# Stick-breaking scans with their second operand in a PSUM bank, and one projection bank in place of two

## Chip, cores and metric

The kernel runs on one core of a Trainium2 chip. The metric is the device time of one execution in microseconds (us): the median of 3 runs was 3153.06 us, from 3152.79 to 3157.4. A core has a matrix engine (TensorE, PE in the profile, with its weight loads as PEld), VectorE (DVE), ScalarE (ACT), GpSimd (POOL) and DMA queues that SyncE (SP) and others feed. Each engine works through its own instructions in order and waits on semaphores for the others. SBUF is the on-chip memory. PSUM is the matrix engine's output memory, eight banks of 512 float32 values on each of 128 partitions; VectorE and ScalarE reach it as well.

## What is computed

One decoder layer on 2048 tokens of width 1024, all in float32: modulated RMSNorm, one input projection, forgetting attention on 8 heads beside stick-breaking attention on 8 heads, output projection, then a channel mixer of an up-projection, a causal convolution of width 3, SiLU gating and a down-projection. The change lies in the stick-breaking attention:

```python
def stick_breaking_attention(q, k, v):
    """A[t,s] = sigmoid(z_ts) * prod_{s<j<t} (1 - sigmoid(z_tj)), s < t, in log space. q,k,v: (B,H,S,Dh)."""
    ...
        z = jnp.einsum('bhqd,bhkd->bhqk', q_blk, k, preferred_element_type=jnp.float32) * scale
        strict = kpos[None, :] < qpos[:, None]
        log_one_minus_beta = jnp.where(strict, jax.nn.log_sigmoid(-z), 0.0)
        rest = lax.cumsum(log_one_minus_beta, axis=3, reverse=True) - log_one_minus_beta
        log_a = jax.nn.log_sigmoid(z) + rest
        a = jnp.where(strict, jnp.exp(log_a), 0.0)
        return jnp.einsum('bhqk,bhkd->bhqd', a.astype(v.dtype), v)
```

For each query row the product of the factors 1 - sigmoid(z) runs from the diagonal to the left. The kernel forms it with a scan over the keys in reversed order.

## The kernel before

**Units.** The attention is cut into 32 units: stick-breaking ("sb") head pairs 0 to 3 with four token blocks of 512 each are units 0 to 15, forgetting ("fox") ones units 16 to 31. A unit has two things to do. Its *projection* (`proj`, `finish_proj`) makes q, k and, for even head pairs, v of two pairs. Its *attention* (`Unit`, `Head`, `SbItem`, `Group`) goes through the unit's queries against all earlier keys.

**Projection.** q and k are each one accumulation group of 24 matmuls of 512 columns (`accumulate`, L268) into a bank that `pj()` hands out; v is two groups of 48 matmuls of 256 columns (L310). A finished group is read from its bank first by ACT (a copy that rounds to the matrix format, L278 or L44) and then by DVE (the remainder, L279 or L45), for V twice each. Only then is the bank free. Pool `psa` has two such banks, so one group can be read out while the next accumulates.

**Stick-breaking attention.** For each head, each of two 128-row query blocks and each chunk of up to 512 keys, `SbItem.weights` does: two matmuls for the logits into a `qk` bank (L368, L369); two sigmoids on ACT, one into a row strip `rw` and one into `a` (L457, L458); the scan on DVE over `rw`, from right to left, in place; and the product `a * rw` shifted by one on POOL (L471). The head's last chunk holds the diagonal (L463): its second operand is the constant `edge`, which is zero but for an identity matrix in its last 128 columns, and the operation is multiply and then maximum, so that the running product starts at 1 on each row's diagonal. Every other chunk (L466) starts from the neighbour's leftmost value and only multiplies; the second operation is "bypass", and the second operand, which doesn't enter the result, is `rw` itself. `Group.turn` then transposes `a` on PE (L383) into a `pt` bank, ACT and DVE read it out (L387, L388), and `Group.add` multiplies with V on PE (L398).

**The stage.** Units 0 to 2 are attended with short strips (`r`); units 3 to 15 follow with `long_rows` set, in one call of `attend`, which looks up to two items ahead, while `fill_proj` advances the projections of units 4 to 16 in step with the attention. After it the fox stage begins with `attend(plan[16:], 2, 2)`. PSUM then holds `psb` (2 `qk`, 3 `pt`, 1 `pv`) and `psa` (2 `pj`). The order in which instructions stand on each engine is not that of the code alone: the framework's scheduler places them by priority and by its own estimate of when each is ready, buffers included, so a change in the number of buffers moves instructions on every engine.

Of the kernel before, what the change touches and what calls it, by code (L numbers as in the profile page):

```python
# [11 lines left out]
AF = mybir.ActivationFunctionType  # L12
ALU = mybir.AluOpType
PSUM = bass.MemoryType.PSUM
# [9 lines left out]
TB = 512  # L24
# [9 lines left out]
def kernel(ctx: ExitStack, tc: tile.TileContext, x, c, w_ada, b_ada, g_attn, w_in, b_fgate,  # L34
                      g_out_fox, g_out_sb, w_out, g_mlp, w_up, conv_w, conv_b, w_down, g_final, out):
    nc = tc.nc
# [28 lines left out]
    edge = const.tile([P, TB + 1], F32, name="edge")  # L65
# [67 lines left out]
    def open_pool(name, side=None, space=None):  # L133
        st = pools[name] = ExitStack()
        kw = dict(space=space) if space is not None else {}
        return st.enter_context(tc.tile_pool(name=name, bufs=1, side=side, reuse_waits="tile", **kw))

    def close_pool(*names):
        for name in names:
            pools.pop(name).close()  # L140

    psb = open_pool("psb", space=PSUM)
    psa = open_pool("psa", side="right", space=PSUM)
# [5 lines left out]
    def bank(pool, tag, bufs):  # L149
        return pool.tile([P, 512], F32, name=f"ps_{tag}", tag=tag, bufs=bufs)  # L150

    pj = lambda: bank(psa, "pj", 2)
    qk = lambda: bank(psb, "qk", 2)
    pt = lambda: bank(psb, "pt", 3)
    pv = lambda: bank(psb, "pv", 1)
# [210 lines left out]
    def logits(cw, qcols, hl, Q, K):  # L366
        b = qk()
        nc.tensor.matmul(b[:, :cw], Q[:, hl, 0, qcols], K[:, hl, :cw], start=True, stop=False)  # L368
        nc.tensor.matmul(b[:, :cw], Q[:, hl, 1, qcols], K[:, hl, :cw], start=False, stop=True)  # L369
        return b  # L370
# [57 lines left out]
    class SbItem:  # L428
# [14 lines left out]
        def weights(self, qi):  # L443
            head, ch = self.head, self.ch
            last = ch == head.n - 1
            need = min(512, (2 * head.j + qi + 1) * P - ch * 512)
            b = logits(max(need, 2 * P), head.qcols(qi), head.hl, head.Q, head.K[ch])
            if last:
                head.right = getattr(head, "right", [None, None])
                if long_rows:  # L450
                    head.right[qi] = sx.tile([P, S + 1], F32, name="rw", bufs=3)
            if long_rows:
                r = head.right[qi][:, ch * 512:ch * 512 + need + 1]
            else:
                r = sx.tile([P, 512 + 1], F32, name="r", bufs=7)
            self.at[qi] = a = sx.tile([P, 512], F32, name="a", bufs=7)
            nc.scalar.activation(r[:, :need], b[:, :need], AF.Sigmoid)  # L457
            nc.scalar.activation(a[:, :need], b[:, :need], AF.Sigmoid, scale=-1.0)  # L458
            if last:

                nc.gpsimd.memset(r[:, need:need + 1], 0.0)
                rev = r[:, 0:need + 1][:, ::-1]
                nc.vector.tensor_tensor_scan(rev, rev, edge[:, TB - need:TB + 1][:, ::-1], 0.0, ALU.mult, ALU.max)  # L463
            elif long_rows:
                rev = r[:, 0:need][:, ::-1]
                nc.vector.tensor_tensor_scan(rev, rev, rev, r[:, need:need + 1], ALU.mult, ALU.bypass)  # L466
            else:
                nc.gpsimd.tensor_copy(r[:, need:need + 1], head.right[qi][:, 0:1])
                rev = r[:, 0:need + 1][:, ::-1]
                nc.vector.tensor_tensor_scan(rev, rev, rev, 1.0, ALU.mult, ALU.bypass)  # L470
            nc.gpsimd.tensor_mul(a[:, :need], a[:, :need], r[:, 1:need + 1])  # L471
            if not long_rows:
                head.right[qi] = r
# [290 lines left out]
    def fill_proj(target, limit=len(units)):  # L764

        while stock and made[0] < limit and taken[0] < target:
            if next(stock[0], StopIteration) is StopIteration:
                stock.pop(0)
                made[0] += 1
                continue  # L770
            taken[0] += 1
# [24 lines left out]
    def unit_proj(i):  # L796
        yield from proj_gen(units[i], xt0 if i == 0 else None)

    psc = p2a = ex = None
    wo = []  # L800
    stock = [unit_proj(i) for i in range(len(units))]
    taken = [0]
# [4 lines left out]
    sx = open_pool("sx", side="right")  # L807
# [8 lines left out]
    ex = open_pool("ex", side="right")  # L816
    sx = open_pool("sx", side="right")
    long_rows = True
    base = taken[0]
    goal = 0  # L820
    seen = {}
# [8 lines left out]
    tick(1 << 20)  # L830
    while made[0] <= 16:
        fill_proj(taken[0] + 1)
    close_pool("sx", "ex")
    ex = None
    sx = open_pool("fx", side="right")
    base = taken[0]
    seen = {}
# [270 lines left out]
    for tb in range(NTB):  # L1108
# [21 lines left out]
        for t in range(4):  # L1130
# [4 lines left out]
            r = de.tile([P, 1], F32, name="r_f", bufs=4)  # L1135
# [43 lines left out]
```

## Time and profile before

| quantity | value |
|---|---|
| median of 3 runs | 3153.06 us |
| span of the profiled execution | 3151.1 us, 1.96 us under the median |
| mean granted TensorE clock in the span | 0.979 |
| PE busy in the span | 2971.6 us (94%), 15934 matmuls |
| DVE busy | 2138.4 us (68%) |
| ACT busy | 1655.3 us (53%) |
| POOL busy | 1306.8 us (41%) |
| stick-breaking stage of units 3 to 15 | 268 to 906.5 us |

The profile is of one execution, whose own time is known by its span alone; the 1.96 us beside it are the distance to the median of the runs. In a row for a group of instructions stand the line, the engine, the operation, output and inputs by the program's names, the shapes and the count, then the busy time in us and the mean of one in ns, and behind a second bar the idle time of the engine just before them with what ended it. A row of waits reads: who waited for whom, us in all, times, longest. A row of stretches gives the busy time of each engine from one point to another, with the number of instructions, and then the granted clock, the share of the DMA engines and GB/s. A row of the timeline begins with start and duration in us. Matmuls are pipelined and their ends are modelled, so a row of several matmuls runs a little into the next; distances from start to start are the ones to use.

### The profile page before, as it was taken

How to read it: one execution, taken by the hardware profiler on the slowest of the kernel's cores; microseconds unless marked ns; L12 is line 12 of the kernel's file. 1: busy time of each engine (PE TensorE's matmuls, PEld its weight loads, DVE VectorE, ACT ScalarE, POOL GpSimd, SP SyncE). 2: the span in 40 equal slices, each digit the busy share in tenths (PEclk: the TensorE clock that was granted, in tenths of full speed). 3: DMA queues.
4: the chain of work that ended last, by engine and by line, in shares of the span. 5: the costliest groups of instructions: out<-in, count | busy, mean ns of one | idle time of the engine just before them, and what ended most of it. 6: DMA issues, size and time to landing. Idle time of an engine off the chain costs nothing.

```text
span 3151.1 us, 46387 instructions
## 1 busy us (share of the span) xinstructions
PE 2971.6 (94%) x15934; PEld 2517.7 (80%) x15934; DVE 2138.4 (68%) x3422; ACT 1655.3 (53%) x3033; POOL 1306.8 (41%) x1459
## 2 busy tenths in 40 slices
PE   7889898989989999999999999999899998999998
PEld 5778797878878889887877778888678887888887
DVE  6776689787976776556743577777987776254253
ACT  5565577666765565556743444444544444343332
POOL 2673566666653242242212244444444442332321
PEclk8999999999999999999999999999999999999999
DMA  9439633654236685685546632222222223554552
GB/s 266 169 133 300 193 106 97 215 180 134 76 115 213 219 288 180 185 301 169 170 153 219 213 96 85 83 88 85 84 81 82 87 86 123 190 201 158 192 200 90
DMA packets 292939, 496.51 MB, mean 158 GB/s; under 512 B 29448, under 2 KB 177664, under 8 KB 291680
## 3 DMA queue, kind: packets, MB, share of 16 engines
q1 hardware_dynamic: 281072, 480.92, 47.9%
q10 hardware_dynamic: 11632, 12.63, 1.1%
q8 instruction: 126, 2.06, 0.3%
q14 instruction: 109, 0.89, 0.1%
HBM read 352.61 MB, written 90.51 MB: 141 GB/s over the span
## 4 chain that ended last, share of the span: by engine, by line
PE 51%; DVE 14%; DMA 13%; POOL 9%; issue 7%; ACT 4%; SPq 2%; POOLq 0%; DVEq 0%; ACTq 0%
PE ps_pj L268 8%; PE ps_o L1118 8%; PE ps_pv L398 6%; PE ps_pt L383 5%; PE ps_pj L310 5%; PE ps_o L968 4%; PE ps_t L1118 4%; PE ps_bc L1118 4%; DMA wuraw<-in_w_up_dram 3%; PE ps_qk L368 3%; DVE wu L45 3%; PE ps_qk L369 3%; DMA hp<-hs 2%; DVE u L1037 2%; POOL ws L956 2%
## 5 line engine op out<-in xcount | busy, mean ns | idle before, releaser
L968 PE MATMUL ps_o<-oa,wu 128*128 128x512 f32 x2088 | 502.7, 392 | 12.6 <-DVE oa L45 5.8
L968 PEld LDWEIGHTS ps_o<-oa,wu 128*128 128x128 f32 x2088 | 391.1, 188 | 102.5 <-DVE oa L45 9.6
L398 PE MATMUL ps_pv<-at,V 128*128 128x256 f32 x2304 | 437.8, 300 | 21.3 <-DVE at L388 8.8
L388 DVE TENSOR_TENSOR at<-ps_pt,at 128x512 fp32r<-128x512 f32 (+1 forms) x576 | 365.1, 650 | 122.4 <-ACT at L387 119.6
L268 PE MATMUL ps_pj<-hp,w_qk 128*128 128x512 f32 x1512 | 417.2, 407 | 17.7 <-DMA hp<-hs 5.5
L387 ACT ACTIVATE at<-ps_pt 128x512 fp32r<-128x512 f32 (+1 forms) x576 | 319.1, 576 | 193.0 <-PE ps_pt L383 132.5
L471 POOL TENSOR_TENSOR a<-a,rw 128x512 f32<-128x512 f32 (+2 forms) x272 | 317.2, 1176 | 234.8 <-DVE rw L466 68.3
L398 PEld LDWEIGHTS ps_pv<-at,V 128*128 128x128 f32 x2304 | 341.8, 192 | 57.9 <-DVE at L388 18.5
L268 PEld LDWEIGHTS ps_pj<-hp,w_qk 128*128 128x128 f32 x1512 | 276.2, 192 | 73.6 <-DMA hp<-hs 7.2
L45 DVE TENSOR_TENSOR wd<-wdraw,wd 128x1024 fp32r<-128x1024 f32 x88 | 112.7, 1280 | 261.9 <-ACT wd L44 261.8
L45 POOL TENSOR_TENSOR g<-graw,g 128x512 fp32r<-128x512 f32 x84 | 142.7, 1702 | 325.8 <-ACT g L44 325.8
L368 PE MATMUL ps_qk<-K,Q 128*128 128x512 f32 (+2 forms) x640 | 260.7, 408 | 14.9 <-ACT a L458 7.1
L466 DVE TENSOR_TENSOR_SCAN rw<-rw 128x512 f32<-128x512 f32 x168 | 251.4, 1509 | 18.0 <-ACT rw L457 16.9
L1118 PE MATMUL ps_o<-wd,g 128*128 128x512 f32 x1040 | 251.1, 391 | 8.7 <-ACT g L44 8.7
L968 PE MATMUL ps_t<-ob,wu 128*128 128x512 f32 x984 | 244.0, 393 | 0.0
L310 PE MATMUL ps_pj<-w_v,hp 128*128 128x256 f32 (+1 forms) x1536 | 230.8, 293 | 9.8 <-DVE V L45 4.6
L369 PE MATMUL ps_qk<-K,Q 128*128 128x512 f32 (+2 forms) x640 | 236.7, 371 | 0.0
L1118 PEld LDWEIGHTS ps_o<-wd,g 128*128 128x128 f32 x1040 | 196.2, 189 | 49.9 <-ACT g L44 9.1
L44 ACT ACTIVATE wu<-wuraw 128x512 fp32r<-128x512 f32 x214 | 133.2, 626 | 195.8 <-PE ps_o L968 132.4
L383 PE MATMUL ps_pt<-edge,a 128*128 128x128 f32 x1088 | 189.8, 280 | 43.0 <-POOL a L471 37.5
L310 PEld LDWEIGHTS ps_pj<-w_v,hp 128*128 128x128 f32 x1536 | 209.8, 195 | 17.3 <-issue 8.7
L968 PEld LDWEIGHTS ps_t<-ob,wu 128*128 128x128 f32 x984 | 187.0, 190 | 39.4 <-ACT hf_m L873 0.2
(222 smaller groups left out, 5753.7 us busy)
## 6 DMA issues: line engine op xcount, KB each, us to landing
hp<-hs SPq DMA_DIRECT2D x224, 512.0 KB
wuraw<-in_w_up_dram SPq DMA_DIRECT2D x84, 512.0 KB
wdraw<-in_w_down_dram SPq DMA_DIRECT2D x84, 512.0 KB
Q<-q SPq DMA_DIRECT2D x128, 256.0 KB
g<-u SPq DMA_DIRECT2D x42, 512.0 KB
graw<-g SPq DMA_DIRECT2D x84, 256.0 KB
hs<-hp SPq DMA_DIRECT2D x32, 512.0 KB
K<-q SPq DMA_DIRECT2D x128, 128.0 KB
```

Of the source, the lines that this page charges most:

```text
L45: (lo_engine or nc.gpsimd).tensor_sub(lo, src, f(hi))
L268: nc.tensor.matmul(acc, w[kt][:, a, n], h[:, bb], start=kt == 0 and i == 0, stop=kt == KT - 1 and i == 2)
L310: nc.tensor.matmul(av[:, t * width:(t + 1) * width], hts[kt][:, a, tok], w[1][kt][:, bb, 0:width], start=kt == 0 and m == 0, stop=kt == KT ...
L368: nc.tensor.matmul(b[:, :cw], Q[:, hl, 0, qcols], K[:, hl, :cw], start=True, stop=False)
L369: nc.tensor.matmul(b[:, :cw], Q[:, hl, 1, qcols], K[:, hl, :cw], start=False, stop=True)
L383: nc.tensor.transpose(b[:, i * P:(i + 1) * P], self.blk(self.kts[kk], qi), ident)
L387: nc.scalar.activation(at[:, 0, lo:], b[:, lo:], AF.Copy)
L388: nc.vector.tensor_sub(at[:, 1, lo:], b[:, lo:], f(at[:, 0, lo:]))
L398: nc.tensor.matmul(o[:, 0:2 * P], head.V[kt // 4][:, kt % 4, head.hl, :], rhs, start=self.first and kk == 0 and w == 0, stop=self.last and ...
L471: nc.gpsimd.tensor_mul(a[:, :need], a[:, :need], r[:, 1:need + 1])
L968: nc.tensor.matmul(b, w[:, p, j], o[:, q], start=first and i == 0, stop=last and i == 2, skip_group_check=True)
L1118: nc.tensor.matmul(banks[t][n], g[:, a, t * P:(t + 1) * P], w[:, b, n * TB:(n + 1) * TB], start=k == 0 and i == 0, stop=k == NKD - 1 and i ...
```

## The change

While the stage of units 3 to 15 runs, pool `psa` is closed and opened anew with one projection bank and one bank `edge_bank`, into which ACT copies the first 512 columns of the strip `edge`. All scans of the stage read their second operand from that bank. The scans of the diagonal chunk lose one element each (its result was a zero that is still written by POOL's memset); that part applies to units 0 to 2 too, which go on reading `edge` in SBUF. After the stage `psa` is opened with two projection banks again.

```diff
-    pj = lambda: bank(psa, "pj", 2)
+    pj = lambda: bank(psa, "pj", 1 if edge_bank is not None else 2)
...
             if last:
 
                 nc.gpsimd.memset(r[:, need:need + 1], 0.0)
-                rev = r[:, 0:need + 1][:, ::-1]
-                nc.vector.tensor_tensor_scan(rev, rev, edge[:, TB - need:TB + 1][:, ::-1], 0.0, ALU.mult, ALU.max)
+                rev = r[:, 0:need][:, ::-1]
+                strip = edge if edge_bank is None else edge_bank
+                nc.vector.tensor_tensor_scan(rev, rev, strip[:, TB - need:TB][:, ::-1], 0.0, ALU.mult, ALU.max)
             elif long_rows:
                 rev = r[:, 0:need][:, ::-1]
-                nc.vector.tensor_tensor_scan(rev, rev, rev, r[:, need:need + 1], ALU.mult, ALU.bypass)
+                nc.vector.tensor_tensor_scan(rev, rev, edge_bank[:, 0:need], r[:, need:need + 1], ALU.mult, ALU.bypass)
...
-    psc = p2a = ex = None
+    psc = p2a = ex = edge_bank = None
...
     long_rows = True
+    close_pool("psa")
+    psa = open_pool("psa", side="right", space=PSUM)
+    edge_bank = bank(psa, "edge", 1)
+    nc.scalar.activation(edge_bank, edge[:, 0:TB], AF.Copy)
...
-    close_pool("sx", "ex")
-    ex = None
+    close_pool("sx", "ex", "psa")
+    ex = edge_bank = None
+    psa = open_pool("psa", side="right", space=PSUM)
```

The instruction order of the two programs differs at most places of the stage. Two places show what kind of difference it is. The first is on PE, at the projections of unit 11, where its k group (L268) ends and its first V group (L310) begins. Before:

```order
L268 MATMUL ps_pj<-hp,w_qk 128x512 x7
L368 MATMUL ps_qk<-K,Q 128x256
L369 MATMUL ps_qk<-K,Q 128x256
L268 MATMUL ps_pj<-hp,w_qk 128x512 x3
L310 MATMUL ps_pj<-w_v,hp 128x256 x6
L368 MATMUL ps_qk<-K,Q 128x512
```

With the change, at the same switch:

```order
L268 MATMUL ps_pj<-hp,w_qk 128x512 x8
L383 MATMUL ps_pt<-edge,a 128x128 x4
L368 MATMUL ps_qk<-K,Q 128x512
L369 MATMUL ps_qk<-K,Q 128x512
L368 MATMUL ps_qk<-K,Q 128x384
L369 MATMUL ps_qk<-K,Q 128x384
L383 MATMUL ps_pt<-edge,a 128x128 x7
L398 MATMUL ps_pv<-at,V 128x256 x9
L310 MATMUL ps_pj<-w_v,hp 128x256 x12
```

Before, the V group follows the k group at once, in the other bank. With the change eleven transposes, two pairs of logits and nine products with V stand between the two groups.

The second place is on PE too, at the end of the stage. Before, unit 17's k group (its last five matmuls are the L268 row) and both its V groups stand ahead of the stage's last stretch of attention:

```order
L268 MATMUL ps_pj<-hp,w_qk 128x512 x5
L310 MATMUL ps_pj<-w_v,hp 128x256 x9
L383 MATMUL ps_pt<-edge,a 128x128 x3
L398 MATMUL ps_pv<-at,V 128x256 x8
L368 MATMUL ps_qk<-K,Q 128x512
```

With the change only unit 17's q group stands ahead of that stretch, and its k group (L268) and V groups (L310) stand behind it, where the last stick-breaking products are:

```order
L368 MATMUL ps_qk<-K,Q 128x256
L369 MATMUL ps_qk<-K,Q 128x256
L383 MATMUL ps_pt<-edge,a 128x128 x2
L398 MATMUL ps_pv<-at,V 128x256
L268 MATMUL ps_pj<-hp,w_qk 128x512 x19
L398 MATMUL ps_pv<-at,V 128x256 x3
L383 MATMUL ps_pt<-edge,a 128x128 x6
L398 MATMUL ps_pv<-at,V 128x256 x4
L268 MATMUL ps_pj<-hp,w_qk 128x512 x5
L310 MATMUL ps_pj<-w_v,hp 128x256 x13
```

So 24 matmuls of 512 columns and 96 of 256 have moved from ahead of the last stretch to behind it.

## Prediction

> **What bounds the kernel now.** I read the page first, then busy time by stretches, then who waited for whom, then single lines. The change acts in one stage, the stick-breaking attention of units 3 to 15 with its projections, from 268 to 906.5 us.
>
> ```profile
> span 3151.1 us, 46387 instructions
> core 0: us, PE busy (x) PEld busy (x) DVE busy (x) ACT busy (x) POOL busy (x), PEclk, DMA share, GB/s
> 268.00:491.00 223.00, 212.97 (x1364) 190.28 (x1363) 177.62 (x218) 145.53 (x311) 123.80 (x159) 0.98 0.60 185
> 491.00:543.00 52.00, 39.18 (x271) 32.86 (x270) 51.94 (x61) 41.10 (x86) 39.03 (x41) 1.00 0.29 92
> 543.00:678.00 135.00, 134.34 (x839) 119.00 (x838) 104.90 (x137) 87.50 (x193) 78.95 (x111) 1.00 0.67 210
> 678.00:726.00 48.00, 33.96 (x181) 27.25 (x179) 40.37 (x39) 35.34 (x75) 42.55 (x41) 0.85 0.31 91
> 738.00:828.00 90.00, 88.76 (x636) 82.27 (x635) 73.68 (x101) 61.45 (x139) 48.90 (x78) 1.00 0.47 140
> 828.00:906.50 78.50, 61.04 (x394) 50.58 (x392) 78.03 (x88) 60.56 (x123) 58.11 (x58) 0.96 0.13 40
> 268.00:906.50 638.50, 582.25 (x3740) 512.68 (x3738) 535.74 (x650) 435.84 (x934) 397.22 (x489) 0.97 0.48 149
> ```
>
> The stage is two things in turn. Where projections run beside the attention (268 to 491, 543 to 678, 738 to 828) PE is busy 95 to 99.5% of the time, and a faster VectorE is worth almost nothing. In three stretches of attention alone (491 to 543, 678 to 726, 828 to 906.5) PE stands idle for 12.8, 14.0 and 17.5 us, 44.3 of the stage's 56.3, and DVE is full (51.94 of 52, 40.37 of 48, 78.03 of 78.5). What PE waits for in those stretches:
>
> ```profile
> PE ps_pt L383 <- POOL a L471: 36.3, 33, 3.0
> PE ps_pt L383 <- POOL a L471: 13.9, 12, 1.5
> ```
>
> The first row is the whole stage, the second the last stretch: the transposes wait for GpSimd's product, which waits for the scan. Now the scans themselves.
>
> ```profile
> L466 DVE TENSOR_TENSOR_SCAN rw<-rw x168: 1251/1334/2170, 269.7 to 904.4; 128x512 f32<-128x512 f32 x168
> L463 DVE TENSOR_TENSOR_SCAN rw<-rw,edge x104: 395/939/2100, 268.2 to 892.3; 128x129 f32<-128x129 f32 x26, 128x257 f32<-128x257 f32 x26, 128x385 f32<-128x385 f32 x26, 128x513 f32<-128x513 f32 x26
> L466 DVE TENSOR_TENSOR_SCAN rw<-rw 128x512 f32<-128x512 f32 x168 | 251.4, 1509 | 18.0 <-ACT rw L457 16.9
> L463 DVE TENSOR_TENSOR_SCAN rw<-rw,edge 128x513 f32<-128x513 f32 x26 | 37.2, 1433 | 11.1 <-ACT rw L457 9.8 <-POOL rw L461 0.5 <-ACT a L458 0.5
> L463 DVE TENSOR_TENSOR_SCAN rw<-rw,edge 128x385 f32<-128x385 f32 x26 | 30.2, 1161 | 3.0 <-ACT rw L457 2.4 <-POOL rw L461 0.5
> L463 DVE TENSOR_TENSOR_SCAN rw<-rw,edge 128x257 f32<-128x257 f32 x26 | 19.0, 732 | 2.9 <-ACT rw L457 2.5 <-POOL rw L461 0.3
> L463 DVE TENSOR_TENSOR_SCAN rw<-rw,edge 128x129 f32<-128x129 f32 x26 | 17.5, 673 | 2.8 <-ACT rw L457 2.8
> L388 DVE TENSOR_TENSOR at<-ps_pt,at 128x512 fp32r<-128x512 f32 x190 | 124.4, 673 | 19.6 <-ACT at L387 18.1
> 850.00 2.17 DVE L466 TENSOR_TENSOR_SCAN rw<-rw 128x512 f32<-128x512 f32 x1
> 849.99 1.09 POOL L471 TENSOR_TENSOR a<-a,rw 128x512 f32<-128x512 f32 x1
> L471 POOL TENSOR_TENSOR a<-a,rw 128x512 f32<-128x512 f32 x194 | 257.3, 1334 | 166.2 <-DVE rw L466 68.3 <-ACT a L458 20.4 <-ACT at L387 20.3
> ```
>
> One shape of the same instruction takes 1251 ns at best and 2170 at worst. The pair at 850 shows a pattern: a product of 1.09 us on POOL begins with a scan, and that scan takes 2.17 us, about 1.09 more than a free one. Products stretch too (mean 1334 ns). L388, beside the same POOL work but with one operand in PSUM, keeps to 673 ns. So the excess looks like a clash of two engines over SBUF operands, which a scan that reads one from PSUM might escape.
>
> **The change, part by part.** *Scans.* A PSUM-fed scan is in no trace. Its price lies between the 0.67 us of L388, a two-operand instruction of that width with one operand in PSUM, and the 1.51 us of today, should nothing clash less. I take 1251 ns, since it is the same scan undisturbed, and L388 shows no surcharge for PSUM. The saving counts where DVE sets the pace:
>
> ```profile
> 491.00:543.00 52.00, 27.00 (x18) 1.00 0.29 92
> 678.00:726.00 48.00, 22.74 (x15) 0.85 0.31 91
> 828.00:906.50 78.50, 45.95 (x30) 0.96 0.13 40
> ```
>
> These are L466 alone: 63 scans, 95.69 us, and 63 x 1.251 is 78.8: 16.9 us less. The three stretches also hold about 24 scans of L463 (272 scans in the stage, 104 of them L463; I take the same mix). On a straight line from 395 ns at 129 elements to 1251 at 512 their four shapes would take 395, 681, 967 and 1253 ns; today's means exceed that by 278, 51, 194 and 180, on average 176: 24 x 0.176 = 4.2 us. Together **-21.1 us**, within the 44.3 us that PE idles there. Ends: 0 where the scans stay as they are; at 0.67 us a scan the 63 alone would save 53, of which PE's idle leaves room for 44.3. After them ACT is next (60.56 of 78.5).
>
> [...]
>
> *One projection bank for two.* Each accumulation group (24 or 48 matmuls) must now be read out by ACT and DVE before the next starts. Two evacuations as they run today, a q and a V:
>
> ```profile
> 445.53 0.71 PE L268 MATMUL ps_pj<-hp,w_qk 128*128 128x512 f32 x2
> 446.65 0.60 ACT L278 ACTIVATE q<-ps_pj 128x512 fp32r<-128x512 f32 x1
> 447.39 0.67 DVE L279 SCALAR_TENSOR_TENSOR q<-ps_pj,q 128x512 fp32r<-128x512 f32 x1
> 775.59 0.84 PE L310 MATMUL ps_pj<-w_v,hp 128*128 128x256 f32 x5
> 778.81 0.40 ACT L44 ACTIVATE V<-ps_pj 128x256 fp32r<-128x256 f32 x1
> 780.39 0.39 DVE L45 TENSOR_TENSOR V<-ps_pj,V 128x256 fp32r<-128x256 f32 x1
> ```
>
> The first row at 445.53 holds a group's last matmul and the next group's first; the last ends near 445.9 and DVE is done at 448.06, so **2.1 us**. The V takes from 776.43 to 780.78, **4.35 us**. Counted along the changed program order, the stage has 36 such switches: 3 follow back to back, 23 behind a q or k group have attention between (the first excerpt above), and 10 come behind a V group. What the attention between them occupies:
>
> ```profile
> 795.54 0.60 PE L383 MATMUL ps_pt<-edge,a 128*128 128x128 f32 x4
> 795.89 0.48 PE L368 MATMUL ps_qk<-K,Q 128*128 128x512 f32 x1
> 796.45 0.60 PE L383 MATMUL ps_pt<-edge,a 128*128 128x128 f32 x4
> 451.23 0.63 PE L398 MATMUL ps_pv<-at,V 128*128 128x256 f32 x4
> 451.70 0.60 PE L383 MATMUL ps_pt<-edge,a 128*128 128x128 f32 x4
> ```
>
> Start to start, four transposes take 0.35 us, a pair of logits 0.56, four products with V 0.47. The excerpt's 11 transposes, 2 pairs and 9 products are 0.96 + 1.12 + 1.06 = 3.1 us: more than 2.1, so the 23 cost nothing that I count. Behind V the filler by the same prices is 3.1 to 4.3 us against 4.35, of which a shorter scan ahead on DVE takes 0.3 off; one of the ten falls into a long piece of attention. I put 0.5 on each of 9, **+4.5**. The 3 bare ones pay 2.1 each, **+6.3**. Ends: 0, and everything bare, 26 x 2.1 + 10 x 4.35 = 98 us. Behind a waiting projection matmul PE's own queue stands: transposes and logits that ACT, DVE and POOL then lack.
>
> *Copy of the strip, pools.* One ACT copy of 512 elements (0.60 us as L278's), behind unit 3's last V evacuation: **+0.6**, at most the 4.35 of an evacuation. SP's and POOL's queues are passed by nothing new; the last scan's missing element is 2 ns.
>
> *Unit 17's k and V move behind the stage* (second excerpt): 24 x 0.23 + 96 x 0.12 us = 17 us of PE work leaves 738 to 828, where PE is 98.6% busy, for the fox stage, where it is as full. Moved between two full places it costs **0**; had it filled PE's idle time before, it would cost the 17. In exchange some five parts more of attention run alone at the end, and as many fewer earlier.
>
> **Sum.** -21.1 + 4.5 + 6.3 + 0.6 = -9.7: a span of 3141.4 for 3151.1. The median shown is 3153.06, 2.0 above the span; with the same 2.0 around it, **3143 us**, -0.3%. A measurement of this kernel can tell about 0.2%, 6.3 us, from no change.
>
> **The rivals.**
> *The switches are not covered* (the other side). At a switch PE needs its filler ready, and the filler waits for the same ACT and DVE that must clear the bank. The mechanism sits at PE's first matmul of each group. Against it: in 543 to 678 and 738 to 828 DVE has 20% to spare. For it: the filler's transposes are the very ones that wait for POOL today. The gain is gone when the 33 filled switches cost (21.1 - 6.3 - 0.6)/33 = 0.43 us each; slower by 6.3 us begins at 0.62. At half of an evacuation, (23 x 2.1 + 10 x 4.35)/33/2 = 1.4 us, they cost 46 in place of 4.5: +32, 3185 us. That it just cancels the gain (3147 to 3159) I hold as likely as that it goes beyond.
> *The scans do not shorten.* If today's stretch came from anything but the second SBUF operand, the change does not do what it says: +11.4, 3164 us; with half of the saving, should a PSUM operand have a surcharge of its own, 3154. The pair at 850 speaks against the first, L388 against the second.
> *Better than counted.* POOL's products shrink to 1.09 us too, the waits of the transposes (36.3 us) go entirely, and all switches hide: -36.3 + 0.6, 3117 us. Against it: DVE stays the busiest engine of those stretches.
>
> **How the numbers follow.** The forecast, 3143 with its own range 3136 to 3149: 0.42, of which 0.06 lies within 0.2%. Better: 0.15. Switches cancel the gain: 0.17. Switches slower: 0.16. Scans not shorter: 0.10, of which 0.03 within 0.2%. Faster 0.36 + 0.15 = 0.51, same 0.06 + 0.17 + 0.03 = 0.26, slower 0.16 + 0.07 = 0.23. The range runs from the better case's near half to the slower case's near half, 3118 to 3172.
>
> **What would show it.** Right: 512-element scans near 1.25 us with little spread, POOL's products near 1.1, PE's wait for POOL well under 36.3 us, and new waits of PE's projection matmuls for DVE of about 10 us. Wrong: scans at 1.5 or above; or waits of L268 and L310 for DVE's q and V above 20 us; or the fox stage growing by more than the 17 us that it takes over.

## The result, and the profile after

Over four runs each the changed kernel takes **3119.62 us** (3117.99 to 3120.98), the kernel before 3154.23 (3152.79 to 3157.4): a ratio of 0.989 with a 95% interval of 0.9878 to 0.9902, 34.6 us or 1.1% less. The forecast was 3143. The direction is right and the time lies 1.6 us inside the range's lower end (3118); the gain is three and a half times the one worked out. The execution profiled took 3119.64 us.

The head of the changed kernel's page, the span and each engine's busy time:

```profile
span 3117.9 us, 46343 instructions
PE 2964.8 (95%) x15934; PEld 2514.9 (81%) x15934; DVE 2077.4 (67%) x3422; ACT 1650.6 (53%) x3034; POOL 1219.2 (39%) x1459
```

The scans, from the page's groups, the answer by shape and the list of one line's instructions (minimum, median, maximum in ns):

```profile
L467 DVE TENSOR_TENSOR_SCAN rw<-rw,ps_edge x168: 1243/1271/1281, 262.4 to 844.2; 128x512 f32<-128x512 f32 x168
L467 DVE TENSOR_TENSOR_SCAN rw<-rw,ps_edge 128x512 f32<-128x512 f32 x168 | 211.1, 1269 | 26.4 <-ACT rw L457 25.9
L464 DVE TENSOR_TENSOR_SCAN rw<-rw,ps_edge 128x512 f32<-128x512 f32 x26 | 31.5, 1213 | 5.8 <-ACT rw L457 5.8
L464 DVE TENSOR_TENSOR_SCAN rw<-rw,ps_edge 128x128 f32<-128x128 f32 x26 | 10.5, 405 | 3.7 <-ACT rw L457 3.6
L472 POOL TENSOR_TENSOR a<-a,rw x272: 408/1091/1105, 255.8 to 845.6; 128x512 f32<-128x512 f32 x84, 128x128 f32<-128x128 f32 x26, 128x384 f32<-128x384 f32 x26
```

The spread is gone: 1251 to 2170 ns before, 1243 to 1281 now, and GpSimd's product, up to 2318 ns before, never takes more than 1105. That the excess comes from GpSimd the timelines of the two engines show. In the kernel before, 22 of the 168 scans have no GpSimd instruction beside them and take 1273 to 1286 ns (mean 1279); the other 146 average 1543. With the change 34 have none (mean 1275), and the 134 that have one average 1267. A GpSimd instruction that only writes stretched nothing here: the two scans of the kernel before that stand beside a memset alone take 1277 and 1284 ns.

The two engines still run side by side. Two rows of the changed kernel's timeline, POOL and DVE (start, length):

```profile
800.87 1.09 POOL L472 TENSOR_TENSOR a<-a,rw 128x512 f32<-128x512 f32 x1 [0.55 <-DVE rw L467]
801.21 1.28 DVE L467 TENSOR_TENSOR_SCAN rw<-rw,ps_edge 128x512 f32<-128x512 f32 x1
```

This scan begins while a product runs and takes 1.28 us, where the scan at 850 of the kernel before took 2.17 beside such a product and ended 1.09 us after it. How the two engines get in each other's way over SBUF no run shows.

Where the time went, by stretches of the changed kernel: up to the stage's first scan, the stage to its last product, then the fox stage to the output projection (stretch, length, busy time and count of PE, PEld, DVE, ACT, POOL, granted clock, DMA share, GB/s):

```profile
0.00:255.20 255.20, 211.54 (x1246) 181.79 (x1246) 176.90 (x308) 153.25 (x343) 133.83 (x172) 0.93 0.65 203
255.20:845.50 590.30, 563.26 (x3643) 494.79 (x3643) 473.75 (x647) 429.97 (x928) 321.56 (x488) 0.99 0.50 155
845.50:1578.90 733.40, 699.67 (x4544) 622.31 (x4542) 472.76 (x1354) 431.62 (x794) 210.98 (x349) 0.98 0.65 206
```

And the same three stretches of the kernel before, cut at the same events:

```profile
0.00:268.20 268.20, 220.57 (x1271) 188.91 (x1272) 177.40 (x309) 153.27 (x342) 134.20 (x172) 0.92 0.63 198
268.20:905.70 637.50, 581.39 (x3735) 512.06 (x3734) 534.74 (x649) 435.28 (x933) 397.16 (x488) 0.97 0.48 149
905.70:1615.00 709.30, 680.47 (x4428) 600.18 (x4426) 470.07 (x1352) 429.50 (x790) 213.18 (x349) 1.00 0.64 207
```

The three together are 36.1 us shorter, of which 3 are lost again later (the spans differ by 33.2). Length less busy time is PE's idle time: 47.6 to 43.7 us ahead of the stage, **56.1 to 27.0 in it**, 28.8 to 33.7 behind it, 28 us less in all. The other 8 us are PE's busy time: as many matmuls (9434 and 9433) take 1482.4 us before and 1474.5 after, with a granted clock of 0.92 and 0.97 before, 0.93 and 0.99 after in the first two stretches. The fox stretch grew by 24 us, 19 of them PE's busy time and 5 its idle time; unit 17's matmuls had been counted at 17.

The stage's idle time is where the forecast put it. The changed kernel's stretches without a projection matmul:

```profile
488.80:523.70 34.90, 31.88 (x211) 25.98 (x211) 34.76 (x47) 30.69 (x67) 22.23 (x32) 1.00 0.21 46
673.40:685.50 12.10, 11.68 (x83) 10.12 (x81) 11.78 (x17) 11.00 (x24) 7.87 (x11) 1.00 0.21 45
694.20:708.00 13.80, 11.48 (x76) 9.37 (x75) 12.09 (x20) 11.68 (x32) 10.78 (x26) 0.99 1.05 327
771.30:845.60 74.30, 67.22 (x440) 54.28 (x439) 73.97 (x96) 65.32 (x136) 47.64 (x62) 1.00 0.05 11
```

DVE is as full as before, but a matmul now stands for 0.169 us of the last stretch (74.3 over 440) where it stood for 0.199 (78.5 over 394). The middle stretch, 48 us of attention alone, became two of 26 us together. What PE waited for in the changed stage:

```profile
PE ps_pj L268 <- DVE q L279: 8.3, 3, 6.6
PE ps_pt L383 <- POOL a L472: 4.9, 15, 0.7
PE ps_pj L310 <- DVE q L45: 2.0, 1, 2.0
PE ps_pj L268 <- DVE V L45: 1.1, 2, 0.8
PE ps_pj L268 <- DVE q L45: 0.2, 1, 0.2
```

The wait for GpSimd's product fell from 36.3 to 4.9 us. The projections' waits for DVE are 11.6 us in all, where the kernel before had 7.5; one of them, 6.6 us, is more than half. It ends at 359.19, and ACT's timeline of the changed kernel shows its cause:

```profile
355.22 0.63 ACT L222 ACTIVATE fe<-fz 32x512 f32<-32x512 f32 x1 [3.69 <-DMA fz<-zs]
355.87 1.28 ACT L223 ACT_TABLE_LOAD   x1
357.16 0.63 ACT L223 ACTIVATE fe<-fe 32x512 f32<-32x512 f32 x1
357.81 0.60 ACT L278 ACTIVATE q<-ps_pj 128x512 fp32r<-128x512 f32 x1
```

The q that holds the only bank (L278) stands on ACT behind the fox gates (L222), which wait 3.69 us for a DMA. A second bank covers such a wait: in the kernel before, this q group ends near 350.3 and is read out as late, at 358.10, but PE works on the k group in the other bank from 353.11.

### The profile page after: what moved, and what is told of

Same layout as the page of the kernel before. It is cut to its first block, busy times and chain, and to the rows that moved or that the text cites. A ratio compares the mean times of both kernels' runs of the same rounds, so it can differ in the third digit from the quotient of the medians.

```text
span 3117.9 us, 46343 instructions
## 1 busy us (share of the span) xinstructions
PE 2964.8 (95%) x15934; PEld 2514.9 (81%) x15934; DVE 2077.4 (67%) x3422; ACT 1650.6 (53%) x3034; POOL 1219.2 (39%) x1459
## 3 DMA queue, kind: packets, MB, share of 16 engines
q1 hardware_dynamic: 281072, 480.92, 48.9%
## 4 chain that ended last, share of the span: by engine, by line
PE 55%; DVE 14%; DMA 11%; POOL 8%; issue 7%; ACT 4%; SPq 1%; POOLq 0%; DVEq 0%; ACTq 0%
PE ps_pj L268 9%; PE ps_o L1124 8%; PE ps_pv L398 6%; PE ps_pt L383 5%; PE ps_pj L310 5%; PE ps_o L974 4%; PE ps_t L1124 4%; PE ps_bc L1124 4%; DMA wuraw<-in_w_up_dram 3%; PE ps_qk L368 3%; PE ps_qk L369 3%; PE ps_o L735 3%; DVE wu L45 3%; DMA hp<-hs 2%; DVE u L1043 2%
## 5 line engine op out<-in xcount | busy, mean ns | idle before, releaser
L268 PE MATMUL ps_pj<-hp,w_qk 128*128 128x512 f32 x1512 | 416.7, 408 | 30.3 <-DMA hp<-hs 11.6
L388 DVE TENSOR_TENSOR at<-ps_pt,at 128x512 fp32r<-128x512 f32 (+1 forms) x576 | 366.0, 652 | 114.3 <-ACT at L387 110.8
L268 PEld LDWEIGHTS ps_pj<-hp,w_qk 128*128 128x128 f32 x1512 | 278.0, 193 | 90.6 <-DMA hp<-hs 15.8
L472 POOL TENSOR_TENSOR a<-a,rw 128x512 f32<-128x512 f32 (+2 forms) x272 | 260.9, 962 | 229.9 <-DVE rw L467 86.5
L310 PE MATMUL ps_pj<-w_v,hp 128*128 128x256 f32 (+1 forms) x1536 | 229.6, 291 | 7.0 <-DVE zn L316 3.7
L467 DVE TENSOR_TENSOR_SCAN rw<-rw,ps_edge 128x512 f32<-128x512 f32 x168 | 211.1, 1269 | 26.4 <-ACT rw L457 25.9
L310 PEld LDWEIGHTS ps_pj<-w_v,hp 128*128 128x128 f32 x1536 | 207.5, 194 | 13.7 <-issue 3.8
L44 ACT ACTIVATE wd<-wdraw 128x1024 fp32r<-128x1024 f32 x88 | 93.0, 1057 | 205.3 <-PE ps_bc L1124 192.7
```

The lines of the kernel that those rows point to most:

```text
L44: nc.scalar.activation(hi, src, AF.Copy)
L268: nc.tensor.matmul(acc, w[kt][:, a, n], h[:, bb], start=kt == 0 and i == 0, stop=kt == KT - 1 and i == 2)
L310: nc.tensor.matmul(av[:, t * width:(t + 1) * width], hts[kt][:, a, tok], w[1][kt][:, bb, 0:width], start=kt == 0 and m == 0, stop=kt == KT ...
L388: nc.vector.tensor_sub(at[:, 1, lo:], b[:, lo:], f(at[:, 0, lo:]))
```

## The experiments

Each kernel was timed against the kernel before on the same chip, where that took 3153.4 to 3154.6 us. Four theories were set against each other. *A*, the operand: all of the gain comes from the scans' second operand, and the lost bank costs what the forecast said. *B*, the order: much of the gain comes from the changed order of instructions, whatever the scans read. *C*, a form of B: with one projection bank the scheduler fills the switches between projection groups with attention, and less attention is left to run alone. *D*, another form of B: the order moves because the pool is closed and opened again or because the last scan lost an element.

**The change without its operand.** Strip copied, one bank given up, but all scans read SBUF:

```diff
-                strip = edge if edge_bank is None else edge_bank
-                nc.vector.tensor_tensor_scan(rev, rev, strip[:, TB - need:TB][:, ::-1], 0.0, ALU.mult, ALU.max)
+                nc.vector.tensor_tensor_scan(rev, rev, edge[:, TB - need:TB][:, ::-1], 0.0, ALU.mult, ALU.max)
...
-                nc.vector.tensor_tensor_scan(rev, rev, edge_bank[:, 0:need], r[:, need:need + 1], ALU.mult, ALU.bypass)
+                nc.vector.tensor_tensor_scan(rev, rev, rev, r[:, need:need + 1], ALU.mult, ALU.bypass)
```

> The bank is given up and the strip copied as in the change, but all scans of the stage read both operands from SBUF as before. Theory A (the gain is the operand's: scan and product no longer clash): scans near 1.50 us and products near 1.33 us again, the whole gain of 34 us gone, and the price of one bank on top, 5 to 12 us: 3159 to 3166 us. Theory B (the gain is the new order, projections and attention mixed more evenly by the single bank): most of the gain stays, 3120 to 3135 us.

3135.0 us, ratio 0.9933 (0.9918 to 0.9948): 21 us *faster* than before, at the edge of what B expected. Its long scans and its products, by shape:

```profile
L466 DVE TENSOR_TENSOR_SCAN rw<-rw 128x512 f32<-128x512 f32 x168 | 250.4, 1502 | 18.0 <-ACT rw L457 17.6
L471 POOL TENSOR_TENSOR a<-a,rw 128x512 f32<-128x512 f32 x194 | 251.9, 1306 | 166.3 <-DVE rw L466 80.1 <-ACT a L458 17.6 <-DVE rw L463 17.3
```

And the wait of its transposes for the product, in the stage:

```profile
PE ps_pt L383 <- POOL a L471: 23.7, 24, 2.1
```

Both engines' instructions are stretched as before, and still PE waits 12.6 us less for them. A falls as far as the bank's price goes.

**The last scan alone back in SBUF.** Only the first pair of lines of that diff; the order on PE, ACT, POOL and SP is that of the change.

> As the change, but the 104 scans of the diagonal chunks read the strip from SBUF; PE, ACT, POOL and SP have the same instruction order as with the change. Theory A: these 104 scans stretch again (excess 0.18 us each before, 18 of the 61 us of all scans), so about a third of the gain is lost: 3127 to 3133 us. Theory B: the order is the same, so the time is too: 3118 to 3122 us.

3122.78 us, 0.9894 (0.9878 to 0.991), which can't be told from the change (0.989). Its 26 SBUF scans of 512 elements take 1497 ns where the change has 1213:

```profile
L463 DVE TENSOR_TENSOR_SCAN rw<-rw,edge 128x512 f32<-128x512 f32 x26 | 38.9, 1497 | 5.7 <-ACT rw L457 5.6
```

So the diagonal's 104 scans carry some 1 to 3 us of the gain, less than expected and not clear of noise; most of what the operand brings lies in the 168 long ones.

**DVE kept as long as before.** The change, with a copy of 128 columns on DVE behind every scan (272 of 0.265 us each, in the median):

```diff
+            if long_rows:
+                pad = sx.tile([P, P], F32, name="pad", bufs=1)
+                nc.vector.tensor_copy(pad, edge_bank[:, 0:P])
```

> As the change, with one more DVE copy of 128 columns from the PSUM strip (about 0.28 us) after each scan of the stage: DVE has its old load, the products on POOL stay undisturbed. If the gain is DVE's shorter scans: some 86 scans in stretches of attention alone x 0.28 = +24 us and more, 3140 to 3155 us. If it is mostly the shorter products on POOL or the order: under +10 us, below 3130 us.

3131.3 us, 0.9926 (0.9911 to 0.994): some 11 us of the gain are given back, between the two ranges expected. The order is not quite the change's: 80% of PE's instructions in the stage stand in the same sequence (the longest that the two kernels have in common), so a part of the 11 us may be the order's.

**GpSimd kept as long as before.** The change, with a memset of 192 columns behind every product (272 of 0.258 us):

```diff
+            if long_rows:
+                pad = sx.tile([P, 192], F32, name="pad", bufs=1)
+                nc.gpsimd.memset(pad, 0.0)
```

> As the change, with a POOL memset of 192 columns (about 0.26 us) behind each product of the stage: POOL has its old load, the scans on DVE stay short. If the shorter products carry much of the gain (PE's transposes wait for them): +10 to +25 us, 3130 to 3145 us. If DVE's scans carry it: under +5 us, 3118 to 3125 us.

3117.51 us, 0.9878 (0.9861 to 0.9894): nothing is given back, in an order on PE that is 90% the change's. So the load taken off DVE counts, and the load taken off GpSimd does not, as far as these two orders tell. The copies and memsets stand behind the scan and the product: they restore how long each engine is occupied, not how long a chunk takes to pass through both. What that quicker passage is worth is not tested here.

**One projection bank, nothing else.** The kernel before, its pool closed and opened around the stage, with one bank there:

```diff
-    pj = lambda: bank(psa, "pj", 2)
+    pj = lambda: bank(psa, "pj", 1 if one_bank else 2)
...
-    long_rows = True
+    long_rows = one_bank = True
+    close_pool("psa")
+    psa = open_pool("psa", side="right", space=PSUM)
...
```

> The kernel before with one projection bank in the stage of units 3 to 15 and nothing else: no strip, all scans as before, the second bank left empty. Theory C (a single bank makes the scheduler put attention between projection groups, which leaves less attention alone on a full DVE): 3132 to 3140 us, as in the run with the bank given up. Theory D (that run's 20 us came from closing and reopening the pool or from the diagonal scans' missing element, through a different order elsewhere): 3150 to 3165 us.

3145.2 us, 0.9972 (0.9961 to 0.9983): 9 us faster, between the ranges of C and D. Its stretches without projections:

```profile
519.70:546.90 27.20, 19.14 (x137) 16.54 (x137) 27.14 (x31) 19.47 (x43) 16.94 (x21) 1.00 0.27 60
699.80:713.80 14.00, 11.84 (x82) 9.95 (x80) 13.94 (x17) 11.68 (x24) 11.26 (x11) 1.00 0.18 39
722.50:737.60 15.10, 11.30 (x77) 8.98 (x75) 13.90 (x19) 12.13 (x32) 13.38 (x24) 1.00 1.05 327
844.60:893.50 48.90, 36.07 (x237) 30.12 (x235) 46.37 (x52) 37.00 (x75) 35.89 (x34) 0.97 0.21 65
```

PE's two largest waits in its stage:

```profile
PE ps_pt L383 <- POOL a L471: 21.9, 21, 2.1
PE ps_pj L268 <- DVE q L279: 8.8, 4, 6.6
```

Over the stretches PE idles as large a share as before (26.9 of 105.2 us; the prediction's three rows have 44.3 of 178.5), but they are 105 us long. The bank's longest wait is the one behind ACT's gates again. In this kernel the bank's waits cost less than the spread attention brings.

**The pool closed and opened, both banks kept.** The same without the first pair of lines.

> The kernel before with pool psa closed and opened anew at both ends of the stage, still with two projection banks and the old scans. Theory C: 3150 to 3158 us, no change. Theory D: 3130 to 3145 us.

3159.8 us, 1.0016 (1.0001 to 1.0032): slower by some 5 us, just above C's range and the other way than D said. Its wait for GpSimd is 38.3 us:

```profile
PE ps_pt L383 <- POOL a L471: 38.3, 36, 2.2
```

**The last scan one element shorter, nothing else.**

```diff
-                rev = r[:, 0:need + 1][:, ::-1]
-                nc.vector.tensor_tensor_scan(rev, rev, edge[:, TB - need:TB + 1][:, ::-1], 0.0, ALU.mult, ALU.max)
+                rev = r[:, 0:need][:, ::-1]
+                nc.vector.tensor_tensor_scan(rev, rev, edge[:, TB - need:TB][:, ::-1], 0.0, ALU.mult, ALU.max)
```

> The kernel before with only the missing element of the diagonal scans (two projection banks, all operands in SBUF). It splits the 10 us between the run with the bank given up (3135) and the one with a single bank and nothing else (3145). If the missing element itself saves: 130 scans x 2 ns is nothing, so 3151 to 3157 us. If its new instruction order is worth the 10 us: 3141 to 3148 us.

3141.8 us, 0.9965 (0.9953 to 0.9977): 11 us faster, though its scans are stretched as before (1507 ns) and its wait for GpSimd is 31.8 us. An edit worth some 2 ns a scan moved the order and with it the time; 96% of PE's instructions in the stage still stand in the same sequence. The scan also no longer reads the element that GpSimd's memset (L461) writes, but in the kernel before DVE waits only 1.3 us for that memset in the whole stage. D is right to this extent: edits that change little but the order move this kernel by 5 to 11 us.

**The long scans alone back in SBUF.** The second pair of lines of the first diff. Its order on PE is nearer to the change's than that of the first experiment: 98% of the stage's instructions stand in the same sequence, there 96%.

> As the change, but the 168 long scans read both operands from SBUF; only the 104 diagonal ones read the strip in PSUM. The order of instructions is nearly that of the change. If the operand's worth goes by the excess of the scans (43 of 61 us sit in these 168) and totals the 15 us between the run with the bank given up and the change: +10 to +12 us, 3129 to 3132 us. If the operand is worth its full 30 us (as with the strip in a transpose bank): 3138 to 3144 us. If the order alone carries the change: 3118 to 3122 us.

3142.43 us, 0.9965 (0.995 to 0.998), 23 us over the change. Its long scans, by shape:

```profile
L467 DVE TENSOR_TENSOR_SCAN rw<-rw 128x512 f32<-128x512 f32 x168 | 249.6, 1497 | 21.2 <-ACT rw L457 20.3
```

Its wait for GpSimd's product, and behind it its last stretch:

```profile
PE ps_pt L383 <- POOL a L472: 20.4, 20, 1.7
```
```profile
783.60:856.50 72.90, 58.82 (x380) 49.28 (x378) 71.51 (x83) 57.67 (x119) 54.35 (x56) 0.95 0.01 5
```

In nearly as long a last stretch PE does 380 matmuls where the change does 440.

**The strip in a transpose bank** (of three; the projections keep two):

```diff
-    pj = lambda: bank(psa, "pj", 1 if edge_bank is not None else 2)
+    pj = lambda: bank(psa, "pj", 2)
...
-    pt = lambda: bank(psb, "pt", 3)
+    pt = lambda: bank(psb, "pt", 2 if edge_bank is not None else 3)
```

> As the change, but the strip's bank is taken from the transposes (pt 3 to 2) and the projections keep two banks. If the operand's part (15 us between the run with the bank given up and the change) does not depend on the projection banks, and two pt banks cost nothing: 3137 to 3142 us. If single-bank mixing (theory C) is replaced by nothing and two pt banks stall PE: 3145 to 3165 us. Below 3118 us it beats the change.

3122.89 us, 0.9896 (0.9867 to 0.9926): as good as the change, and better than either range expected.

**Two transpose banks, scans as before.** The kernel before with only that bank given up, its pool `psb` closed and opened around the stage.

> The kernel before with two transpose banks for three in the stage, and nothing else (two projection banks, scans as before). Its distance to the run with the strip in the transpose bank (3122.9) is the operand's worth at two projection banks. If two transpose banks cost little: 3153 to 3160 us, operand worth 30 to 37 us. If the fewer banks reorder for the better as the single projection bank did: 3138 to 3148 us, operand worth 15 to 25 us.

3169.19 us, 1.0044 (1.0028 to 1.006): slower than either range. PE's wait for transposes to be read out:

```profile
PE ps_pt L383 <- DVE at L388: 51.4, 57, 1.8
```

The same wait in the kernel with the strip in that bank:

```profile
PE ps_pt L383 <- DVE at L388: 22.2, 45, 1.7
```

With the same banks the operand is worth 46 us here, and of all pairs with and without it this one is the nearest in order: 99% of the stage's instructions stand in the same sequence on PE, on ACT and on GpSimd. DVE's scans stand ahead of the evacuation that frees the scarcer bank, and by the two rows PE waits 29 us longer for it when they are stretched.

**The strip in a logits bank** (one left of two; the diff is that of the strip in a transpose bank, with "qk" cut from 2 to 1 and "pt" left at 3).

> As the change, but the strip's bank is taken from the logits (qk 2 to 1) and the projections keep two banks. Logits then wait for both sigmoids of the part before (about 1.1 us of ACT for each of 272 parts): 3150 to 3200 us. If the waits are covered by other PE work: 3137 to 3142 us.

3314.42 us, 1.0505 (1.0478 to 1.0531), far above what was expected. PE's wait for logits to be read out, about 2 us in the stage before:

```profile
PE ps_qk L368 <- ACT a L458: 37.7, 33, 7.1
```

That row is 38 of some 160 us. Over the whole stage, which here lasts to 1071, PE idles 143 us where it idled 56, and its busy time in the kernel grows to 3039.9 us from 2971.6; what drives the second part is not shown. Of the three kinds of bank this is the one that can't be spared.

**The strip from the first unit on.** In a transpose bank, copied ahead of units 0 to 2, whose scans (r) the change leaves in SBUF:

```diff
-                rev = r[:, 0:need + 1][:, ::-1]
-                nc.vector.tensor_tensor_scan(rev, rev, rev, 1.0, ALU.mult, ALU.bypass)
+                rev = r[:, 0:need][:, ::-1]
+                nc.vector.tensor_tensor_scan(rev, rev, edge_bank[:, 0:need], head.right[qi][:, 0:1], ALU.mult, ALU.bypass)
```

> A version meant to beat both: the strip in a transpose bank from the attention of unit 0 on, so that the 24 inner scans of units 0 to 2 (1.69 us each for 513 elements) and their diagonal ones escape the clash as well, starting from the neighbour's first column. 24 x 0.42 + 24 x 0.2 = 15 us of DVE, in a stretch where PE idles 22 us of 158: 3110 to 3120 us if a third to all of it counts; above 3123 us if two transpose banks hurt there.

3121.75 us, 0.989 (0.9865 to 0.9916): no better than the change. The 24 scans of units 0 to 2 in the change, by shape:

```profile
L471 DVE TENSOR_TENSOR_SCAN r<-r 128x513 f32<-128x513 f32 x24 | 40.5, 1694 | 5.1 <-POOL r L469 3.3 <-ACT r L457 1.0 <-POOL r L461 0.5
```

And in this kernel:

```profile
L471 DVE TENSOR_TENSOR_SCAN r<-r,ps_edge 128x512 f32<-128x512 f32 x24 | 29.8, 1267 | 4.2 <-ACT r L457 4.1
```

Each scan is a quarter shorter, and the time stays. Against the kernel with the strip in a transpose bank (3122.89 us) PE's idle time ahead of the stage fell in the profiled executions, from 48.2 to 41.7 us, but as many matmuls (1273 and 1275) took 220.5 us there for 212.5, at a granted clock of 0.92 for 0.95. Whether the shorter scans bring nothing there or the clock hid it isn't settled. No version is clearly faster than the change.

**All together.** In the profiles of the kernels below the stage's stretches of 8 us or more without a projection matmul were taken in whole microseconds, with the time that PE idles in them:

| projection banks, long scans' operand | runs' ratios | stretches, us | PE idle in them, us | share |
|---|---|---|---|---|
| two, SBUF: before; shorter last scan; pool opened again | 1; 0.9965; 1.0016 | 175; 172; 186 | 43.5; 40.9; 48.9 | 25%; 24%; 26% |
| one, SBUF: one bank; change without operand; long scans in SBUF | 0.9972; 0.9933; 0.9965 | 101; 115; 135 | 26.1; 27.1; 25.0 | 26%; 24%; 19% |
| one, PSUM: the change; last scan in SBUF; longer GpSimd | 0.989; 0.9894; 0.9878 | 130; 136; 119 | 12.4; 16.9; 11.5 | 10%; 12%; 10% |
| two, SBUF, one transpose bank fewer | 1.0044 | 241 | 58.3 | 24% |
| two, PSUM, strip in that bank | 0.9896 | 205 | 27.0 | 13% |
| one, PSUM, longer DVE | 0.9926 | 124 | 21.9 | 18% |

Giving up the bank shortens the stretches, in three orders out of three; the operand lowers the share of them in which PE idles. That is C, and what was right of A. In the whole stage, the bank's new waits included, PE idles 54.9 to 60.5 us in the kernels of the first row, 42.5 to 48.7 in those of the second and 27.0 to 32.5 in those of the third.

By the means of the first three rows, the step from two banks to one is worth 12 us and the operand 22. The first has an uncertainty of about its own size: two edits that change little but the order moved the two-bank kernel 11 us one way and 5 the other. The operand's worth stands clear of that: 46, 23 and 14 us in the three pairs whose orders on PE agree to 99, 98 and 96%, all three the same way, the last alone hardly more than an order can move.

PE's busy time for the kernel's 15934 matmuls moved too: 2971.6 to 2979.3 us in the four kernels with two projection banks and SBUF scans, 2958.9 to 2967.0 in all others but the one short of a logits bank. So the 8 us of the result that are not idle time recur wherever the stage idles less. Why is not shown.

## Why the prediction was right in its direction and wrong in its size

- **The scans' term (-21.1): right.** It took 1251 ns for a PSUM-fed scan; 1243 to 1281 was measured. The nearest pair of orders (long scans in SBUF and the change) gives 23 us, the means of the table 22, the change without its operand 14; with two transpose banks it is 46. Its parts fit less well. The pair at 850 was misread: that scan takes 0.92 us more than a free one, not 1.09. The same mix would have given 63 x 104/168 = 39 diagonal scans; the profile has 24 in those stretches, as the forecast said, but for another reason than it gave, and they exceed its straight line by some 7 us, not 4.2. Of this, all 104 brought 1 to 3.
- **No surcharge for an operand in PSUM: right.** The forecast took it from L388, which reads one operand from PSUM at 673 ns; in the kernel before, a subtraction of the same width with both operands in SBUF, with no GpSimd instruction beside any of its eight, is no shorter:

```profile
L45 DVE TENSOR_TENSOR hp<-hf_a,hp 128x512 fp32r<-128x512 f32 x8 | 5.5, 687 | 4.2 <-ACT hp L44 4.2
```

With no GpSimd instruction beside them the PSUM-fed scans average 1275 ns and the SBUF ones 1279.
- **The switches (+4.5 and +6.3): right in kind, wrong in size and as a loss.** The projections wait 11.6 us for DVE, but the kernel before had 7.5 of that already: 4.1 are new, where the forecast added 10.8. They come less as twelve of 0.5 to 2.1 us than as one of 6.6, behind ACT's queue, which the forecast did not look at.
- **The step that failed** is the one that closes the count of the moved work: "In exchange some five parts more of attention run alone at the end, and as many fewer earlier". It took the amount of attention alone as fixed and priced the bank by its waits alone, so +10.8 us. With one bank the transposes, logits and products that fill each switch are taken out of the stretches of attention alone, where PE idles a quarter of the time: 175 us of such stretches became 101 to 135, and PE's idle time in them fell by 16 to 19 us with the scans still in SBUF. The one bank alone gave 9 us where the forecast had +11.4 for it and the copy: taken at their word, these are 20 of the 25 us by which the gain was undercounted (34.6 for 9.7), though 9 us is no more than an order can move. The order shown at unit 11's switch had the filling in it; the forecast read in it what covers the wait and did not ask where it came from. It also priced PE's idle time alone, and put the 8 us of PE's busy time at nothing.
- **The middle stretch was misread.** The forecast called DVE full from 678 to 726, at 40.37 us of 48. POOL was fuller, at 42.55, and held two kinds of work:

```profile
L45 POOL TENSOR_TENSOR w_v<-raw_v,w_v 128x256 fp32r<-128x256 f32 x8 | 9.5, 1190 | 0.0
L45 POOL TENSOR_TENSOR w_qk<-raw_qk,w_qk 128x256 fp32r<-128x256 f32 x5 | 6.2, 1249 | 1.2 <-ACT w_qk L44 1.2
```

These, of the kernel before in that stretch, are weight preparations; with the change six of them take 743 ns each between 673 and 708:

```profile
L45 POOL TENSOR_TENSOR w_qk<-raw_qk,w_qk 128x256 fp32r<-128x256 f32 x6 | 4.4, 743 | 0.5 <-ACT w_qk L44 0.5
```

They clash with the scans as the products do (five long scans of the kernel before that stand beside such a preparation alone average 1436 ns), and the forecast did not count them: 13 at 743 ns would take 9.7 us in place of 15.7. What that was worth on the path no run separates; with GpSimd lengthened again all over the stage nothing was lost.
- **Unit 17's k and V moved behind the stage at no cost: right to about 7 us.** The fox stretch grew by 24 us for 17 us of matmuls, and growth beyond the 17 was one of the prediction's own signs of being wrong. Whether the 7 belong to the move or to the new order there isn't settled.
- **The rivals.** "Better than counted" named the time (3117) and two of its three reasons: products at 1.09, and the wait for them nearly gone. Its third, that the switches hide, does not hold as put: they cost, and the stretches that they shorten repay it. The range holds the result by this rival's time, which set its lower end, and not by the forecast's own sum. The objection raised against it, that DVE stays the busiest engine of these stretches, is true (73.97 of 74.3 us) and was no objection. "The scans do not shorten" and "the switches are not covered" are refuted by the rows above.

Open: how much of the bank's 9 to 21 us would stay in yet another order. The three kernels with one bank and SBUF scans are alike in the stretches (101 to 135 us) and their idle time (25.0 to 27.1), but their times lie 12 us apart, and those of the two-bank kernels of the first row 16.

## What to carry to other kernels

Where an instruction's time spreads over a factor of 1.7 at one shape, look for the neighbour that shares its operands' memory before counting the instruction itself; one operand moved to the other memory may end the clash for both (here 1509 ns became 1269 for the scan and 1334 became 1093 for the product). A buffer taken away is not priced by its new waits alone: ask what the scheduler puts into the gaps and which starved stretch it takes that from. And where a scheduler sets the order, time one or two edits that change little but the order first, since below their spread no single pair of kernels tells a cause.

## What the runs showed of the hardware

A DVE scan with one operand in PSUM and one in SBUF ran beside GpSimd's SBUF work with a spread of 1243 to 1281 ns over 168 instructions and showed no surcharge: with no GpSimd instruction beside it, it averaged 1275 ns where both operands in SBUF gave 1279. The same scan with both operands in SBUF averaged 1479 to 1511 in the seven kernels that had it, whatever the order; the two of the kernel before that stood beside a GpSimd memset alone, which only writes, took 1277 and 1284 ns. GpSimd is the other loser of the clash, by as much: the products of 512 elements average 1334 ns before and 1093 with the change, and its preparations of w_qk, at most 757 ns in the changed stage, took up to 1725. At 405 ns for 128 elements and 1213 for 512 the diagonal's PSUM-fed scan costs 2.1 ns an element and about 135 ns besides.
